# A hybrid attention and recurrence block: tables spread beside the recurrence, heads' weights split beside its last chunk, weights laid out by group

## The chip, the cores and the metric

The kernel runs on one core of a Trainium2 chip. The metric is the device time of one execution, in microseconds (us). TensorE (PE) does the matrix products, VectorE (DVE), ScalarE (ACT) and GpSimd (POOL) the elementwise work, and SyncE (SP) issues every DMA transfer of this kernel, on one queue. Each engine works through its own instructions in order; semaphores tie the engines together.

## What is computed

One block of a network acts on 2048 latent tokens (32 rows by 64 columns of a grid) and 256 context tokens, all of width 1024, in float32. Cut to its core:

```python
shift, scale, gate = split(silu(c) @ w_mod + b_mod, 3)      # same for the context, from c_ctx
h  = rms_norm(x, norm_g) * (1 + scale) + shift              # hc likewise
q, k, v, z_a, u, z_l = split(h @ w_in, ...)                 # w_in: 1024 x 3072, six groups of 512 columns
# group A: 8 heads of 64, neighbourhood attention (8 rows x 16 columns) plus all context keys
s_loc = where(col_mask, rope(norm(q)) @ rope(norm(k)) / 8 + rpb[head, dr, dc], -1e30)
attn  = softmax(concat[s_loc, norm(q) @ norm(k_ctx) / 8]) @ concat[v_band, v_ctx]
# group B: 8 blocks of 64, a convolution and a recurrence in both directions
uc = depthwise_conv(u) + conv_b
r, i = sigmoid(uc @ w_a + b_a), sigmoid(uc @ w_x + b_x)     # block-diagonal weights, per direction
a = exp(-8 * r * softplus(-lam)); b = sqrt(1 - a * a) * i * uc
y = scan(a, b, forward) + scan(a, b, backward)              # h_t = a_t * h_(t-1) + b_t
out = x + gate * (concat[attn * silu(z_a), y * silu(z_l)] @ w_out)
```

## The kernel before

Products that need float32 accuracy are made of float16 pairs: an operand is split into a high part (`hh`, `wh`) and a low part (`hl`, `wl`), and three products are added, high by high, low by high and high by low (L345 to L347 for channels by tokens, L604 to L606 for tokens by channels).

A weight group goes through two steps. `wload` brings 128 or 192 columns of `w_in` into a float32 tile `wraw` (L312, one DMA for each piece of columns, so three for a head's q, k and v). `wsplit` then finds its largest magnitude (a reduction on VectorE, L320, a transpose and a spread of it over the partitions by two small operations of TensorE, L112 and L115, with VectorE's L114 and L117 between), makes a power of two of it, and writes `wh` on ScalarE (L325) and `wl` on VectorE (L326).

The program runs in stages:

- The modulation vectors come from `w_mod`; then the context's 256 tokens and four blocks of 512 latent tokens are normalised, transposed on TensorE (L283), scaled on ScalarE into `h` (L286) and split into `hh` and `hl` (L288, L290).
- `tables` builds the attention's bias tables: the relative position bias `rp`, scaled, goes to DRAM (`d_r`, then `d_f`, which is first filled with the masking value NEG from the tile `ng`), comes back as `tu` and `tw`, is rearranged by ScalarE into `te` (L665 to L668) and written to DRAM as four tables `d_t`. From there 24 DMAs from DRAM to DRAM spread them into the three tables `d_e` that the heads read (L675), parts of which two DMAs fill with NEG (L677).
- `u_proj` makes the recurrence's input for a chunk of 128 channels, with the convolution (into `uc`).
- `lru` runs the recurrence for chunks 0 to 3. It loads the gates' weights into `gw` (L421, L424), splits them into `gh` and `gl` (L427, L428), and for each direction computes two gates for five stretches of tokens (three products each, L448 to L450, tanh at L452), the coefficients (L453 to L460) and the scans (L462, L469). `gw` takes one of two buffers of the tag "z", which the tiles `sz` of the next item use too.
- Beside each direction of a chunk, two of the four blocks of a z group are projected (`z_units`; tanh L480, `sz` L481, stored at L566 and L567) and, after the first direction, the next z group's weights are loaded and split. `gate` sums the output's gate vector from eight loads `wg` of `w_mod` (L584, L587, L589).
- After the last chunk the weights of heads 0 and 1 are loaded and split, head 0 is projected, and then the eight heads' attention runs, with the next head's projection beside it. The output projection ends the program.

The order of instructions on each engine isn't the order of the code: a scheduler places all instructions by a model of their times, by their dependences, and by priorities from the order in which the code issues them (`issue_after` makes what follows wait in that order for a given instruction). A DMA is placed on SP's queue in the same way. A transfer's semaphore is one of eight that are used in turn, so no more than eight transfers are outstanding.

Of the kernel before, what the change touches and what calls it, by code (L numbers as in the profile page):

```python
# [7 lines left out]
F32 = mybir.dt.float32  # L8
# [9 lines left out]
D = 1024  # L18
S = 2048
CTX = 256  # L20
NH = 8
HD = 64
AW = 512
LW = 512
KC = 8
# [3 lines left out]

NV = 5  # L30

CQ, CK, CV, CZA, CU, CZL = 0, 512, 1024, 1536, 2048, 2560

R_BM, R_G, R_C, R_CC, R_CW, R_CB, R_BA, R_BX, R_LAM, R_N = 0, 24, 32, 40, 48, 64, 68, 76, 84, 92
ROWS = ("b_mod", "norm_g", "c", "c_ctx", "conv_w", "conv_b", "lru_ba", "lru_bx", "lru_lam")
# [24 lines left out]
class K:  # L60
# [237 lines left out]
            return [self.wp["l"].tile([128, KC, 128], F16, tag=x, name=x, bufs=1) for x in ("wh", "wl")]  # L298
        return [self.wp["h"].tile([128, KC, 192], F16, tag=x, name=x, bufs=2)[:, :, 0:n] for x in ("wh", "wl")]

    def wload(self, parts, tag):

        n = sum(w for _, w in parts)
        wp = self.wp["z" if tag == "z" else "h"]
        if tag == "z":
            raw = (self.p0 or wp).tile([128, KC, n], F32, tag="raw", name="wraw", bufs=2 if self.p0 else 1)
        else:
            raw = wp.tile([128, KC, 192], F32, tag="raw", name="wraw", bufs=1)[:, :, 0:n]
        wv = self.a["w_in"].rearrange("(k p) n -> p k n", p=128)
        o = 0  # L310
        for c, w in parts:
            self.nc.sync.dma_start(raw[:, :, o:o + w], wv[:, :, c:c + w])  # L312
            o += w
        return raw, n, tag

    def wsplit(self, raw, n, tag, early=False):
# [13 lines left out]
        nc.vector.tensor_tensor(osc, inv, self.ial, ALU.mult)  # L330
        return wh, wl, osc

    def wgroup(self, parts, tag, slow=False, early=False):
        raw = self.wload(parts, tag)
        with ExitStack() as st:
            if slow:
                st.enter_context(self.tc.issue_after(self.hh_op.ins))
                st.enter_context(self.tc.issue_after(self.hl_op.ins))
            return self.wsplit(*raw, early)
# [72 lines left out]
    def lru(self, c, uc, p, fill):  # L412


        nc, a = self.nc, self.a
        N = CTX + S
        t = lambda x: p.tile([128, N], F32, tag=x, name=x, bufs=2)
        A, X = t("A"), t("X")
        gl = p.tile([128, 4, 128], F32R, tag="gl", name="gl", bufs=1)
        gw = self.zp.tile([128, 512], F32, tag="z", name="gw", bufs=2).rearrange("p (g c) -> p g c", g=4)  # L420
        nc.gpsimd.memset(gw, 0.0)  # L421
        for g, nm in enumerate(("lru_wa", "lru_wx")):
            for f in range(2):
                nc.sync.dma_start(gw[64 * f:64 * f + 64, 2 * g:2 * g + 2, 64 * f:64 * f + 64],  # L424
                                  a[nm][:, 2 * c + f].rearrange("d i j -> i d j"))
        gh = p.tile([128, 4, 128], F32R, tag="gh", name="gh", bufs=1)
        nc.vector.tensor_copy(gh, gw)  # L427
        nc.vector.tensor_tensor(gl, gw, gh.bitcast(F32), ALU.subtract)  # L428

        I = t("I")  # L430
        uh = p.tile([128, N], F32R, tag="uh", name="uh", bufs=1)
        ul = p.tile([128, N], F32R, tag="ul", name="ul", bufs=1)
        done = []
        for d in range(2):
            if d:
                A, X, I = t("A"), t("X"), t("I")
            kc = slice(4 * d + c, 4 * d + c + 1)
            for b in (0, CTX, CTX + 512, CTX + 1024, CTX + 1536):
                m = 512 if b else CTX
                s = slice(b, b + m)  # L440
                u = uc[:, s]
                if d == 0:
                    nc.scalar.copy(uh[:, s], u)  # L443
                    nc.gpsimd.tensor_tensor(ul[:, s], u, uh[:, s].bitcast(F32), ALU.subtract)  # L444
                for g, dst in enumerate((X, I)):
                    w = 2 * g + d
                    q = self.any_bank()[:, :m]
                    nc.tensor.matmul(q, gh[:, w, :], uh[:, s], start=True, stop=False)  # L448
                    nc.tensor.matmul(q, gh[:, w, :], ul[:, s], start=False, stop=False)
                    nc.tensor.matmul(q, gl[:, w, :], uh[:, s], start=False, stop=True)  # L450
                    k = 8 * g + 4 * d + c
                    nc.scalar.activation(dst[:, s], q, AF.Tanh, bias=self.hb[:, k:k + 1], scale=0.5)  # L452
                nc.vector.scalar_tensor_tensor(I[:, s], I[:, s], 1.0, u, ALU.add, ALU.mult)  # L453
            for h in range(2):
                s = slice(N // 2 * h, N // 2 * (h + 1))
                nc.scalar.activation(A[:, s], X[:, s], AF.Exp, bias=self.nk4[:, kc], scale=self.nk4[:, kc])
                nc.vector.scalar_tensor_tensor(I[:, s], A[:, s], 1.0, I[:, s], ALU.add, ALU.mult)
                nc.scalar.activation(X[:, s], X[:, s], AF.Tanh, bias=self.k2[:, kc], scale=self.k2[:, kc])
            nc.scalar.activation(X, X, AF.Sqrt, scale=0.25)
            nc.vector.tensor_tensor(X, X, I, ALU.mult)  # L460
            if d == 0:
                nc.vector.tensor_tensor_scan(A, A, X, 0.0, ALU.mult, ALU.add)  # L462
            done.append(A)
            fill(d)
        F, A = done
        init = 0.0
        for o, m in ((0, CTX), (CTX + S // 2, S // 2), (CTX, S // 2)):
            r = lambda x: x[:, o:o + m][:, ::-1]
            nc.vector.tensor_tensor_scan(r(A), r(A), r(X), init, ALU.mult, ALU.add)  # L469
            init = A[:, o:o + 1]  # L470
            if o:
                nc.gpsimd.tensor_tensor(F[:, o:o + m], A[:, o:o + m], F[:, o:o + m], ALU.add)
                nc.sync.dma_start(self.d_y[128 * c:128 * c + 128, o - CTX:o - CTX + m], F[:, o:o + m])
# [10 lines left out]
    def phase1(self, left, right):  # L484
        nc, a = self.nc, self.a
# [13 lines left out]
        with ExitStack() as s1:  # L499
# [2 lines left out]
            ug = {}  # L502

            def u_group(c, g=None):
                wh, wl, osc = g or self.wgroup([(CU + 128 * c, 128)], "z", slow=c > 1)
                if g:
                    osc = self.small(1, F32, "wo")
                    nc.vector.tensor_tensor(osc, g[2], self.ial, ALU.mult)
                cw = self.small(4, F32, f"cw{c % 2}")
                nc.vector.tensor_scalar(cw, self.vec[:, R_CW + c:R_CW + 16:4], osc, None, ALU.mult)  # L510
                return wh, wl, cw
# [10 lines left out]
            with ExitStack() as s0:  # L522
# [1 line left out]
                mods = self.mods(p0)  # L524
                next(mods)
                with self.tc.issue_after(self.last.ins):
                    g0 = self.wgroup([(CU, 128)], "z", early=True)
                xs = next(mods)
                with self.tc.issue_after(self.last.ins):
                    self.prep(p0, 2, 1, hhc, hlc, xs, True)  # L530
# [4 lines left out]
                    for tb in range(4):  # L535
# [1 line left out]
                        if tb < 3:  # L537
                            nxt = self.prep_in(p0, a["x"], 4, tb + 1)
                        self.prep(p0, 4, 0, self.hh[tb], self.hl[tb], xs)
                    with ExitStack() as s3:  # L540
                        self.tables(self.pool(s3, "tab", side="right"))
                    self.softplus(p0)
                    ucs = [u_proj(0), u_proj(1)]
# [3 lines left out]

            def z_group():
                c = len(za)
                g = self.wgroup([(CZA + 128 * c, 128)], "z", slow=c > 0)  # L550
                nc.vector.tensor_scalar(self.zs[:, c:c + 1], g[2], 0.5, None, ALU.mult)
                za.append(g)
            self.wp["h"] = self.pool(self.wright, "w2", bufs=2, side="right")
            with ExitStack() as s2:
# [4 lines left out]
                def z_units(c, d):  # L559
# [9 lines left out]
                    if d == 0 and c < 3:  # L569
                        z_group()  # L570

                for c in range(4):
                    self.lru(c, ucs[c], p, lambda d, c=c: z_units(c, d))
                    if c < 2:
                        ucs.append(u_proj(c + 2))

# [32 lines left out]
    def tables(self, q):  # L609
# [26 lines left out]
        nc.sync.dma_start(d_r, rp)  # L636
        d_f = self.drm.tile([16, 2, NH, 15, 32], F32, name="d_f")
        ng = q.tile([128, 864], F32, name="ng")
        nc.gpsimd.memset(ng, NEG)
        ff = d_f.rearrange("q t h k c -> (q t h k c)").rearrange("(p n) -> p n", p=128)  # L640
        for i in range(2):
            nc.sync.dma_start(ff[:, 480 * i:480 * i + 480], ng[:, 0:480])
# [7 lines left out]
        for t in range(3):  # L650
# [8 lines left out]
            for r in range(4):  # L659
                e = q.tile([128, 1024], F32, tag="te", name="te", bufs=2)  # L660
                for tab, o, g in ((u, 0, 5), (w, 640, 3)):
# [5 lines left out]
                    else:  # L667
                        nc.scalar.copy(eo, ti)  # L668
                nc.sync.dma_start(d_t[r][t], e)

        self.d_e = [self.drm.tile([2, NH, 64, 3, w], F32, name=f"d_e{i}") for i, w in enumerate(BW)]

        def spread(rt, f, r, o, src, n):
# [1 line left out]
            nc.sync.dma_start(e, d_t[r][:, :, src:src + n].rearrange("t p w -> p t w"))  # L675
        for f, o in ((0, 256), (1, 0)):
            nc.sync.dma_start(self.d_e[2 * f][f].rearrange("h (c r) t w -> (h c) (r t) w", r=4)[:, :, o:o + 128],  # L677
                              ng[:, 0:128].unsqueeze(1).broadcast_to([128, 12, 128]))
        for r in range(4):
            for f in range(2):  # L680
                spread(1, f, r, 0, 128 * (1 - f), 512)
# [1 line left out]
            spread(0, 0, r, 0, 768, 256)  # L683
            spread(2, 0, r, 0, 128, 384)
            spread(2, 1, r, 128, 640, 256)

    def bias_load(self, p, h, rt):

# [41 lines left out]
        self.nc.gpsimd.memset(v[:, :, 1, 64:66], 0.0)  # L730

    def head_w(self, n):
        return self.wload([(CQ + HD * n, HD), (CK + HD * n, HD), (CV + HD * n, HD)], "h")

    def head_bank(self, n):

# [185 lines left out]
    def phase2(self, left, right):  # L922
# [5 lines left out]
        with ExitStack() as sg:  # L928
# [13 lines left out]
                nc.gpsimd.memset(x[:, :, 64:128], 0.0)  # L942
            self.zero = self.const.tile([128, 1], F32, name="zero")
            nc.gpsimd.memset(self.zero, 0.0)
            self.hw, self.bias, self.o = {}, [], {}
            with self.tc.issue_after(self.last.ins):
                for i in range(2):
                    self.hw[i] = self.wsplit(*self.head_w(i))
                for H in self.head_proj(0, p, q):
                    pass  # L950
            lz = self.lru_gate()
# [23 lines left out]
    def lru_gate(self):  # L975

        nc = self.nc
        for c in range(4):
            hsc = self.zs[:, 4 + c:5 + c]

            raw = self.wload([(CZL + 128 * c, 128)], "h" if c == 3 else "l")
            yield
            wh, wl, osc = self.wsplit(*raw)
            nc.vector.tensor_scalar(hsc, osc, 0.5, None, ALU.mult)
# [158 lines left out]
```

## Time and profile before

| | us |
|---|---|
| median of 3 runs | 1267.96 (1267.69 to 1269.3) |
| the profiled execution | 1268.18 |
| its span | 1266.4 |
| TensorE busy | 1116.4 (88%) |
| VectorE busy | 926.4 (73%) |
| ScalarE busy | 618.0 (49%) |
| GpSimd busy | 472.2 (37%) |

The profile is of one execution. Its span runs from the first instruction to the last; 1.8 us of the measured time lie outside of it. A share of busy time is a mean over all stages, so a stage is read by its own stretch: normalising x from about 59 to 121 us, the first two `u_proj` to 150, the recurrence from 168 to about 420, head 0's projection to 460, attention and output to the end. `PEclk` is the granted clock of TensorE as a share of full speed.

### The profile page before, as it was taken

What the parts mean: (1) busy time and instruction counts of PE and PEld (TensorE: products, weight loads), DVE (VectorE), ACT (ScalarE), POOL (GpSimd) and SP (SyncE); (2) the same over time, 40 slices, a digit from 0 to 9 for tenths busy, and PEclk for the clock granted to TensorE, in tenths of its full rate; (3) what the DMA queues carried; (4) which work ended last, traced back from release to release, by engine and by line L of the source; (5) the groups of instructions that cost most, each with busy time, mean ns of one, the idle gap of its engine ahead of it and who ended that gap; (6) DMA issues with size and microseconds to landing.
All of it is one profiled execution on the core that took longest, in us unless ns stands there. A gap on an engine that the chain in (4) does not pass through costs nothing. (4 is left out here: it accounts for less than half of the span.)

```text
span 1266.4 us, 26204 instructions
## 1 busy us (share of the span) xinstructions
PE 1116.4 (88%) x9964; PEld 854.8 (67%) x9964; DVE 926.4 (73%) x2548; ACT 618.0 (49%) x1189; POOL 472.2 (37%) x861
## 2 busy tenths in 40 slices
PE   7767658996985959999999999999998997999997
PEld 1434324453543857899878988789887876888786
DVE  7898556869688667888978988788888874554432
ACT  1697118283588125655646555555555644231200
POOL 0245100403030377566564655646556462000000
PEclk9798869998998888999989999999999998999999
DMA  9746962111112623344533445335353537436352
GB/s 352 270 165 243 310 193 51 59 46 56 24 30 59 152 35 82 70 104 107 110 83 64 109 92 126 83 66 108 89 122 81 136 93 193 142 101 187 109 153 67
DMA packets 196014, 149.50 MB, mean 118 GB/s; under 512 B 129453, under 2 KB 168109, under 8 KB 195887
## 3 DMA queue, kind: packets, MB, share of 16 engines
q1 hardware_dynamic: 195887, 147.82, 43.6%
q8 instruction: 78, 1.28, 0.4%
q14 instruction: 49, 0.40, 0.1%
HBM read 96.42 MB, written 47.94 MB: 114 GB/s over the span
## 5 line engine op out<-in xcount | busy, mean ns | idle before, releaser
L604 PE MATMUL mm<-wh,hh 128*128 128x192 f16 x960 | 237.0, 247 | 1.7 <-DVE V L762 1.6
L605 PE MATMUL mm<-wl,hh 128*128 128x192 f16 x960 | 236.9, 247 | 0.0
L606 PE MATMUL mm<-wh,hl 128*128 128x192 f16 x960 | 236.9, 247 | 0.0
L895 DVE TENSOR_TENSOR Pl<-pt,Ph 128x384 f16<-128x384 f32 (+1 forms) x256 | 127.9, 517 | 57.2 <-ACT Ph L894 56.4
L345 PE MATMUL mm<-hh,wh 128*128 128x512 f16 x384 | 150.8, 393 | 17.9 <-DVE sz L481 12.0
L346 PE MATMUL mm<-hl,wh 128*128 128x512 f16 x384 | 150.0, 391 | 7.8 <-POOL hl L290 6.9
L887 ACT ACTIVATE SP<-SP,nb 128x640 f32<-128x640 f32 (+1 forms) x128 | 110.4, 880 | 94.2 <-DVE nb L885 89.8
L347 PE MATMUL mm<-hh,wl 128*128 128x512 f16 x384 | 148.7, 388 | 0.7 <-DVE wl L326 0.7
L894 ACT CAST Ph<-pt 128x384 f16<-128x384 f32 (+1 forms) x256 | 107.1, 452 | 79.2 <-PE pt L893 75.3
L893 PE MATMUL pt<-id,SP 128*128 128x128 f32 x704 | 116.9, 283 | 2.4 <-ACT SP L887 1.7
L604 PEld LDWEIGHTS <-hh 128*128 128x128 f16 x1024 | 100.6, 98 | 8.9 <-issue 5.2
L605 PEld LDWEIGHTS <-hh 128*128 128x128 f16 x1024 | 100.6, 98 | 2.8 <-issue 1.6
L606 PEld LDWEIGHTS <-hl 128*128 128x128 f16 x1024 | 100.5, 98 | 0.8
L882 DVE CUSTOM_DVE_ANT_0 SP<-sl,b,m 128x384 f32<-128x384 f32 (+1 forms) x128 | 93.4, 736 | 6.9 <-PE sl L830 6.2
L830 PE MATMUL sl<-qk,qt 128*128 128x128 f16 (+2 forms) x800 | 79.4, 232 | 17.9 <-DMA qk<-ST 8.2
L444 POOL TENSOR_TENSOR ul<-uc,uh 128x512 fp32r<-128x512 f32 (+1 forms) x20 | 30.5, 1553 | 151.0 <-ACT uh L443 150.9
L900 PEld LDWEIGHTS <-Ph 128*128 128x128 f16 x1408 | 79.5, 97 | 9.0 <-ACT Ph L894 2.9
L893 PEld LDWEIGHTS pt<-id,SP 128*128 128x128 f32 x704 | 79.4, 144 | 6.9 <-ACT SP L887 2.8
L346 PEld LDWEIGHTS <-wh 128*128 128x128 f16 x416 | 42.1, 101 | 59.2 <-issue 23.6
L347 PEld LDWEIGHTS <-wl 128*128 128x128 f16 x416 | 41.8, 101 | 56.9 <-issue 17.2
L719 POOL TENSOR_TENSOR ST<-P,ST 128x256 f16<-128x256 f32 x64 | 43.5, 680 | 93.7 <-ACT ST L718 93.4
L900 PEld LDWEIGHTS <-Pl 128*128 128x128 f16 x704 | 66.0, 99 | 17.1 <-DVE Pl L895 11.1
(303 smaller groups left out, 3049.5 us busy)
## 6 DMA issues: line engine op xcount, KB each, us to landing
b<-d_e SPq DMA_DIRECT2D x32, 288.0 KB
wm<-w_mod SPq DMA_DIRECT2D x16, 512.0 KB
x<-x SPq DMA_DIRECT2D x16, 512.0 KB
wraw<-w_in SPq DMA_DIRECT2D x12, 512.0 KB
d_t<-te SPq DMA_DIRECT2D x12, 512.0 KB
d_e<-d_t SPq DMA_DIRECT2D x8, 768.0 KB
wraw<-w_in SPq DMA_DIRECT2D x24, 256.0 KB
b<-d_e SPq DMA_DIRECT2D x16, 384.0 KB
```

What stands on the lines that cost most here:

```text
L345: nc.tensor.matmul(out, wh[:, k, :], hh[:, k, :n], start=(k == 0), stop=False)
L346: nc.tensor.matmul(out, wh[:, k, :], hl[:, k, :n], start=False, stop=False)
L347: nc.tensor.matmul(out, wl[:, k, :], hh[:, k, :n], start=False, stop=(k == KC - 1))
L604: nc.tensor.matmul(out, hh[:, k, t0:t0 + 128], wh[:, k, :], start=(k == 0), stop=False)
L605: nc.tensor.matmul(out, hh[:, k, t0:t0 + 128], wl[:, k, :], start=False, stop=False)
L606: nc.tensor.matmul(out, hl[:, k, t0:t0 + 128], wh[:, k, :], start=False, stop=(k == KC - 1))
L882: nc.vector.tensor_tensor_reduce(SP[:, 0:W], sl[:, 0:W], bt[:, CT[j], 0:W], self.qs, m1, ALU.add, ALU.max, accum_out=m2)
L887: nc.scalar.activation(SP[:, :N], SP[:, :N], AF.Exp, bias=nb)
L893: nc.tensor.transpose(pt[:, i - c0, :], SP[:, 128 * i:128 * i + 128], self.id32)
L894: nc.scalar.copy(Ph[:, c0:c1], pt)
L895: nc.vector.tensor_tensor(Pl[:, c0:c1], pt, Ph[:, c0:c1], ALU.subtract)
L900: nc.tensor.matmul(pv[:, jj], P[:, i, :], v[:, w:w + 66], start=(i == j0 == 0), stop=(i == nch - 1 and j0 == 2))
```

## The change

Four things change.

- `w_in` is handed over in two other layouts, `w_qkv` (a head's q, k and v columns together) and `w_gr` (the other groups of 128 columns), so that each load of a weight group is one DMA with one contiguous run for each partition.
- `tables` is issued behind x's last load. The masking value goes to a small DRAM tile `d_n`, from which the two NEG fills of `d_e` now read.
- The 24 spreads of `d_e` move out of `tables` into a generator of four parts of six, whose parts are issued beside the recurrence, at chunk 0's second direction, both of chunk 1 and the first of chunk 2 (the NEG fills stand at the first part). `gw` gets a buffer of its own.
- The weights of heads 0 and 1 are loaded and split beside chunk 3's two directions, no longer after the recurrence.

```diff
-    def wload(self, parts, tag):
+    def wload(self, src, tag):
...
-        wv = self.a["w_in"].rearrange("(k p) n -> p k n", p=128)
-        o = 0
-        for c, w in parts:
-            self.nc.sync.dma_start(raw[:, :, o:o + w], wv[:, :, c:c + w])
-            o += w
+        self.nc.sync.dma_start(raw, src)
...
-        gw = self.zp.tile([128, 512], F32, tag="z", name="gw", bufs=2).rearrange("p (g c) -> p g c", g=4)
+        gw = p.tile([128, 4, 128], F32, tag="gw", name="gw", bufs=1)
...
-                    with ExitStack() as s3:
+                    with ExitStack() as s3, self.tc.issue_after(self.xld.ins):
                         self.tables(self.pool(s3, "tab", side="right"))
...
+                self.hw = {}
+
+                spread = self.table_spread()
+
+                def fill(c, d):
+                    z_units(c, d)
+                    if (c, d) in ((0, 1), (1, 0), (1, 1), (2, 0)):
+                        next(spread)
+                    if c == 3:
+                        self.hw[d] = self.wsplit(*self.head_w(d))
+
                 for c in range(4):
-                    self.lru(c, ucs[c], p, lambda d, c=c: z_units(c, d))
+                    self.lru(c, ucs[c], p, lambda d, c=c: fill(c, d))
...
+        bneg = self.drm.tile([128, 128], F32, name="d_n")
         nc.gpsimd.memset(ng, NEG)
+        nc.sync.dma_start(bneg, ng[:, 0:128])
...
+    def table_spread(self):
+
+        nc, d_t = self.nc, self.d_t
         self.d_e = [self.drm.tile([2, NH, 64, 3, w], F32, name=f"d_e{i}") for i, w in enumerate(BW)]
...
-                              ng[:, 0:128].unsqueeze(1).broadcast_to([128, 12, 128]))
+                              self.bneg.unsqueeze(1).broadcast_to([128, 12, 128]))
         for r in range(4):
...
             spread(2, 1, r, 128, 640, 256)
+            yield
...
     def head_w(self, n):
-        return self.wload([(CQ + HD * n, HD), (CK + HD * n, HD), (CV + HD * n, HD)], "h")
+        return self.wload(self.a["w_qkv"][n], "h")
...
             with self.tc.issue_after(self.last.ins):
-                for i in range(2):
-                    self.hw[i] = self.wsplit(*self.head_w(i))
                 for H in self.head_proj(0, p, q):
```

The order of the instructions changes with it. First SP's queue, before the change, from the end of the spreads on (`d_e` is a spread, `wg` a load for the gate vector, `gw` the gates' weights, `wraw` a z group's weights):


```order
L675 DMA d_e_1027<-d_t_958 128x3x256
L584 DMA wg<-w_mod 128x1024 x2
L593 DMA grow<-b_mod 1x1024
L424 DMA gw<-lru_wa 64x2x64 x2
L424 DMA gw<-lru_wx 64x2x64 x2
L312 DMA wraw<-w_in 128x8x128
L584 DMA wg<-w_mod 128x1024 x6
L312 DMA wraw<-w_in 128x8x128
```

Here the gates' weights of chunk 0 and then z group 0's and 1's weights stand behind all 24 spreads. With the change SP's queue reads like this where the spreads begin,


```order
L678 DMA d_t_958<-te 128x1024
L688 DMA d_e_1810<-d_t_957 128x3x512
L420 DMA gw<-lru_wa 64x2x64 x2
L678 DMA d_t_959<-te 128x1024
L420 DMA gw<-lru_wx 64x2x64 x2
L678 DMA d_t_960<-te 128x1024
L688 DMA d_e_1810<-d_t_957 128x3x512
L688 DMA d_e_1809<-d_t_957 128x3x384
```

so that chunk 0's `gw` has one spread ahead of it, and like this where they end, with z group 1's weights in the last row:


```order
L688 DMA d_e_1810<-d_t_960 128x3x512
L591 DMA wg<-w_mod 128x1024
L688 DMA d_e_1809<-d_t_960 128x3x384
L688 DMA d_e_1809<-d_t_960 128x3x256
L688 DMA d_e_1811<-d_t_960 128x3x384
L688 DMA d_e_1811<-d_t_960 128x3x256
L309 DMA wraw<-w_gr 128x1024
```

All 24 spreads still stand ahead of z group 1's weights and of the first store of `sz`; z group 0's weights have moved up among them.

Next VectorE where the first z groups are done, before the change (`I` belongs to the recurrence, `sz` to z group 0, the reduction of `wraw` at L320 to z group 1):


```order
L589 SCALAR_TENSOR_TENSOR gacc<-wg,silu,gacc 128x1024
L551 TENSOR_SCALAR zs<-wo 128x1
L589 SCALAR_TENSOR_TENSOR gacc<-wg,silu,gacc 128x1024
L320 TENSOR_REDUCE wm<-wraw 128x1
L481 SCALAR_TENSOR_TENSOR sz<-sz,mm 128x512
L597 TENSOR_TENSOR grow<-grow,pt 1x512
L597 TENSOR_TENSOR grow<-grow,sc 1x512
L453 SCALAR_TENSOR_TENSOR I<-I,uc 128x256
L453 SCALAR_TENSOR_TENSOR I<-I,uc 128x512 x2
L114 TENSOR_REDUCE av<-po 1x1
L481 SCALAR_TENSOR_TENSOR sz<-sz,mm 128x512
L453 SCALAR_TENSOR_TENSOR I<-I,uc 128x512
```

And with the change, where the same steps have the lines L449, L477 and L316:


```order
L477 SCALAR_TENSOR_TENSOR sz<-sz,mm 128x512
L596 SCALAR_TENSOR_TENSOR gacc<-wg,silu,gacc 128x1024
L477 SCALAR_TENSOR_TENSOR sz<-sz,mm 128x512
L596 SCALAR_TENSOR_TENSOR gacc<-wg,silu,gacc 128x1024
L316 TENSOR_REDUCE wm<-wraw 128x1
L114 TENSOR_REDUCE av<-po 1x1
L477 SCALAR_TENSOR_TENSOR sz<-sz,mm 128x512
```

The steps of chunk 0's recurrence that stood between the `sz` are no longer there, and additions to `gacc` stand there instead; z group 1's reduction is still ahead of later `sz`, as it was.

Last TensorE at the end of the recurrence, before the change (L345 to L347 are the last z block, L112 and L115 belong to a head's split, L448 to L450 to the last gate, L604 on to head 0):


```order
L347 MATMUL mm<-hh_108,wl 128x512
L112 MATMUL mm<-id_63,wm 1x128
L448 MATMUL sc<-uh,gh 128x512
L449 MATMUL sc<-ul,gh 128x512
L450 MATMUL sc<-uh,gl 128x512
L115 MATMUL mm<-av,id_63 128x1
L604 LDWEIGHTS hhc
L604 MATMUL sl<-wh,hhc 128x128
L604 LDWEIGHTS hh_104
L604 MATMUL sl<-wh,hh_104 128x192
L605 LDWEIGHTS hhc
```

And with the change, where L343 is the end of the last z block and L611 to L613 are head 0:


```order
L343 LDWEIGHTS wl
L343 MATMUL mm<-hh_108,wl 128x512
L611 LDWEIGHTS hhc
L611 MATMUL sl<-wh,hhc 128x128
L612 LDWEIGHTS hhc
L612 MATMUL sl<-wl,hhc 128x128
L613 LDWEIGHTS hlc
L613 MATMUL sl<-wh,hlc 128x128
```

The split's two steps and the last gate's products are gone from between the last z block and head 0's projection; they stand further up.

## Rows read from the trace of the kernel before

**Rows 1.** Busy time (and count) of each engine in stretches of the span.

```profile
core 0: us, PE busy (x) PEld busy (x) DVE busy (x) ACT busy (x) POOL busy (x), PEclk, DMA share, GB/s
...
59.00:121.00 62.00, 44.05 (x224) 25.66 (x223) 53.88 (x96) 57.28 (x89) 29.95 (x24) 0.91 0.50 173
...
150.00:170.00 20.00, 1.36 (x4) 1.26 (x5) 7.06 (x11) 0.85 (x1) 0.00 (x0) 0.55 0.91 290
170.00:400.00 230.00, 199.42 (x887) 105.03 (x885) 173.79 (x206) 141.65 (x180) 43.74 (x24) 0.93 0.21 57
400.00:414.40 14.40, 1.00 (x4) 0.81 (x5) 13.93 (x18) 11.42 (x11) 0.00 (x0) 0.53 0.09 18
...
460.00:480.00 20.00, 8.05 (x58) 5.86 (x56) 9.99 (x44) 7.28 (x16) 15.97 (x36) 0.66 0.23 46
```

**Rows 2.** TensorE's waits, 140 to 420: who is waited for, us, times, longest.

```profile
PE sl L448 <- DVE gh L427: 22.0, 2, 20.1
PE mm L345 <- DVE sz L481: 12.0, 3, 5.8
PE po L115 <- DVE av L114: 7.5, 1, 7.5
PE mm L115 <- DVE av L114: 7.3, 1, 7.3
PE sl L604 <- ACT wh L325: 4.5, 1, 4.5
...
PE sl L605 <- DVE wl L326: 2.6, 1, 2.6
```

**Rows 3.** TensorE's times: start, us, instruction, idle before it and its releaser.

```profile
148.15 0.38 PE L115 MATMUL po<-av,id 1*128 1x1 f32 x2
168.64 0.58 PE L448 MATMUL sl<-uh,gh 128*128 128x256 f32 x1 [20.12 <-DVE gh L427]
...
178.58 0.39 PE L345 MATMUL mm<-hh,wh 128*128 128x512 f16 x1 [1.67 <-ACT wh L325]
...
398.77 0.40 PE L450 MATMUL sc<-uh,gl 128*128 128x512 f32 x1
...
414.49 0.26 PE L605 MATMUL sl<-wl,hhc 128*128 128x128 f16 x1 [2.56 <-DVE wl L326]
```

**Rows 4.** VectorE's times, at four places.

```profile
168.16 0.42 DVE L427 CAST gh<-gw 128x512 fp32r<-128x512 f32 x1
...
169.23 1.21 DVE L320 TENSOR_REDUCE wm<-wraw 128x1 f32<-128x1024 f32 x1
...
207.34 0.68 DVE L481 SCALAR_TENSOR_TENSOR sz<-sz,mm 128x512 f32<-128x512 f32 x1
...
423.38 0.27 DVE L771 TENSOR_TENSOR rgc<-sl,gs 128x128 f32<-128x128 f32 x1
```

**Rows 5.** SP's times of issue, 0 to 480; the last column is the count.

```profile
49.56 0.35 SPq L636 DMA_DIRECT2D d_r<-rp  x1
...
117.96 36.56 SPq L675 DMA_DIRECT2D d_e<-d_t  x19
...
160.51 3.06 SPq L424 DMA_DIRECT2D gw<-lru_wx  x2
...
180.66 0.38 SPq L312 DMA_DIRECT2D wraw<-w_in  x1
```

**Rows 6.** The spreads, from the view of tile d_e: ns, least, median, most.

```profile
L675 SPq DMA_DIRECT2D d_e<-d_t x24: 618/1690/4050, 111.0 to 152.7; - x24
```

**Rows 7.** ScalarE's times, first h of x and first copy into te.

```profile
58.94 0.78 ACT L286 ACTIVATE h<-pt,sha,Ga 128x512 f32<-128x512 f32 x1 [1.66 <-PE pt L283]
...
73.00 2.57 ACT L668 COPY te<-tu 128x640 f32<-128x640 f32 x2
```

**Rows 8.** VectorE's wl of a head, 400 to 480, groups by form: busy us, mean ns.

```profile
L326 DVE SCALAR_TENSOR_TENSOR wl<-wraw,ws,wh 128x1536 f16<-128x1536 f32 x2 | 3.6, 1817 | 0.3 <-ACT wh L325 0.3
```

More of the change, by code (lines that the diff above doesn't have):

```diff
@@ L30 @@
 NV = 5
-CQ, CK, CV, CZA, CU, CZL = 0, 512, 1024, 1536, 2048, 2560
+GZA, GU, GZL = 0, 4, 8
 R_BM, R_G, R_C, R_CC, R_CW, R_CB, R_BA, R_BX, R_LAM, R_N = 0, 24, 32, 40, 48, 64, 68, 76, 84, 92
@@ L299, in w_tiles @@
         return [self.wp["h"].tile([128, KC, 192], F16, tag=x, name=x, bufs=2)[:, :, 0:n] for x in ("wh", "wl")]
-    def wload(self, parts, tag):
-        n = sum(w for _, w in parts)
+    def wload(self, src, tag):
+        n = src.shape[2]
         wp = self.wp["z" if tag == "z" else "h"]
@@ L331, in wsplit, with wgroup @@
         return wh, wl, osc
-    def wgroup(self, parts, tag, slow=False, early=False):
-        raw = self.wload(parts, tag)
+    def wgroup(self, g, tag, slow=False, early=False):
+        raw = self.wload(self.a["w_gr"][g], tag)
         with ExitStack() as st:
@@ L504, in u_group @@
             def u_group(c, g=None):
-                wh, wl, osc = g or self.wgroup([(CU + 128 * c, 128)], "z", slow=c > 1)
+                wh, wl, osc = g or self.wgroup(GU + c, "z", slow=c > 1)
                 if g:
@@ L526, in phase1 @@
                 with self.tc.issue_after(self.last.ins):
-                    g0 = self.wgroup([(CU, 128)], "z", early=True)
+                    g0 = self.wgroup(GU, "z", early=True)
                 xs = next(mods)
@@ L549, in z_group @@
                 c = len(za)
-                g = self.wgroup([(CZA + 128 * c, 128)], "z", slow=c > 0)
+                g = self.wgroup(GZA + c, "z", slow=c > 0)
                 nc.vector.tensor_scalar(self.zs[:, c:c + 1], g[2], 0.5, None, ALU.mult)
@@ L669, in tables @@
                 nc.sync.dma_start(d_t[r][t], e)
+        self.d_t, self.bneg = d_t, bneg
+    def table_spread(self):
+        nc, d_t = self.nc, self.d_t
         self.d_e = [self.drm.tile([2, NH, 64, 3, w], F32, name=f"d_e{i}") for i, w in enumerate(BW)]
@@ L979, in lru_gate @@
             hsc = self.zs[:, 4 + c:5 + c]
-            raw = self.wload([(CZL + 128 * c, 128)], "h" if c == 3 else "l")
+            raw = self.wload(self.a["w_gr"][GZL + c], "h" if c == 3 else "l")
             yield
@@ L1117 @@
         "x": (S, D), "ctx": (CTX, D),
-        "w_mod": (D, 3 * D), "b_mod": (24, 128), "w_in": (D, 3 * D), "w_out": (D, D),
+        "w_mod": (D, 3 * D), "b_mod": (24, 128), "w_out": (D, D),
         "q_norm_g": (1, HD), "k_norm_g": (1, HD), "rpb": (NH * 15, 31),
@@ L1123 @@
     arrays["vec"] = np.ascontiguousarray(np.concatenate([np.asarray(inputs[n]).reshape(-1, 128) for n in ROWS]).T)
+    w = np.asarray(inputs["w_in"]).reshape(KC, 128, 3 * D).transpose(1, 0, 2)
+    arrays["w_qkv"] = np.ascontiguousarray(w[:, :, :3 * AW].reshape(128, KC, 3, NH, HD).transpose(3, 0, 1, 2, 4).reshape(NH, 128, KC, 3 * HD))
+    arrays["w_gr"] = np.ascontiguousarray(w[:, :, 3 * AW:].reshape(128, KC, 12, 128).transpose(2, 0, 1, 3))
     half = HD // 4
```

2 lines of the change are left out of this document (1 added, 1 removed).

## The prediction, made before the changed kernel had run

> **What bounds the kernel now.** I read the stretch table first, to see which engine is idle where the change works [rows 1]. From 59 to 121 us, where x is normalised, ScalarE is busy 57.28 of 62.00 us: that stretch is ScalarE's. From 150 to 170 TensorE works 1.36 us of 20.00 while the DMA engines are 0.91 busy: a wait on transfers. From 170 to 400 TensorE is busy 199.42 of 230.00, VectorE 173.79, ScalarE 141.65: mostly TensorE's, with 30.6 us of holes. From 400 to 414.4 TensorE does 1.00 us and VectorE 13.93 of 14.40.
>
> The list of TensorE's waits names these holes [rows 2]: 22.0 us for the gates' weights gh (one wait of 20.1), 12.0 for the z blocks' sz, 7.5 and 7.3 at the two ends of the weights' maximum (L115), 4.5 and 2.6 for head 0's wh and wl. TensorE's own times [rows 3] place them: nothing between L115 at 148.15 and the first gate at 168.64; nothing of size between the last gate at 398.77 and head 0's stream at 414.49. SP's times give the reason for the first [rows 5]: 19 spreads are issued from 117.96 on over 36.56 us, and gw's second pair goes out only behind them, at 160.51. VectorE casts it at 168.16 [rows 4]. From 460 to 480 TensorE is again idle 12 us.
>
> **Terms, part by part.**
>
> *Tables behind x's loads.* Two moves oppose each other. x is no longer behind the tables' transfers, so the ScalarE-bound stretch, whose first h is now at 58.94 [rows 7], can begin about 7 us earlier: the four NEG fills that were issued ahead of most of x carry 2.06 MB, 7 us at 290 GB/s [rows 1]. But the table chain starts later. Its first link, d_r, was issued at 49.56, and the first copy into te came at 73.00, 23.4 us behind [rows 5, 7]; now that copy stands in ScalarE's order after block 1's h, and the chain's links come behind all of x. The copies are the same, so ScalarE's sum does not change; what it gains by starting it loses by waiting at the first te. I take 0, between −7 (no wait) and +14 (a wait of 21 us, nearly the chain's whole length, less the 7). The transfer that now carries NEG through DRAM is one of 64 KB on a queue that is not waited for: 0.
>
> *gw in a buffer of its own, its load ahead of the spreads.* The wait of 20.1 goes [rows 2, 3]: −20.1. uc and uh of the context block are ready before, since TensorE's queue named gh alone. gh waited twice, 22.0 in all; the second, 1.9, is of the same kind: −1.9. Together −22.0, and at the least −12 if the next operand is 10 us late.
>
> *What is late next.* The gates now stand together on TensorE and z block 0 behind them. Its weights' split (maximum, L112, L115, wh, wl) had gates around it before: its reduction started at 169.23 [rows 4] and z's first matmul at 178.58 [rows 3], 9.35 us with 24 gates in between. Now those gates are finished when the split runs, in a queue that is served in order. Between 0 (the split overlaps the gates as before) and +9.4 (all bare), I take the middle, +5.
>
> *Spreads beside the recurrence.* The 24 spreads stay on the one SP queue and now stand among gw, wg and the z weights. At 36.56/19 = 1.92 us each [rows 5] they take 46 us; with six 512 KB loads between them, at 290 GB/s [rows 1] about 1.8 us each, 57 us. From about 120 (when the last d_t is written) z block 1's weights land near 177 to 183, where they were issued at 180.66 before [rows 5]. VectorE has z 1's reduction ahead of z 0's third sz. By the terms above VectorE is there near 174 (gates from 148.5, 8 us; split 5; two blocks of 24 matmuls and their sz, 12). It then waits 3 to 9 us, and TensorE, which has one free bank, a part of that. I take +3, between 0 and +9.
>
> *Middle of the recurrence.* No operation is added; 30.6 us of TensorE's holes bound a gain [rows 1], and the order is another. I take 0, between −15 (half the holes) and +15 (as much new).
>
> *Heads' split beside chunk 3.* TensorE's waits of 7.3, 4.5 and 2.6 [rows 2] go, as head 0's weights are ready: from the last gate's start, 398.77, plus 0.4, to 414.49 are 15.3 us [rows 3], −15.3. VectorE could hold that back: it is nearly full there, and reads the first head's sums only at 423.38 [rows 4], behind the scans. What it sheds for certain are the two wl, 3.6 us [rows 8]; that is the least, −4. The most is the 15.3 and the 12 idle us of 460 to 480: −27. The nearest rows are TensorE's own, so −15.3. The moved split's cover is VectorE's 56 idle us of 170 to 400; were there none, it would cost its own 3.6 and the two reductions' about as much.
>
> *Weights by group.* 15 fewer DMAs and longer runs. Of TensorE's waits none names a weight load [rows 2]: 0, at best −2.
>
> Sum: 0 − 22.0 + 5 + 3 + 0 − 15.3 = −29.3. The profiled execution took 1268.18 us, 1.8 of it outside the span; the median of the runs is 1267.96, so 0.2 less changes nothing. Forecast **1239**.
>
> A rule weighed: the clock. In 150 to 170 and 400 to 414.4 the granted clock was 0.55 and 0.53 [rows 1], near the lower level (1.2 of 2.4 GHz), after TensorE had stood still; the first gate, of 256 columns, took 0.58 us where a late one, of 512, took 0.40 [rows 3]. The Trainium skill, "TensorE: Matmul & The Clock Gate", Part 1, says that the gate falls to half rate when the array idles and that work opens it again. By it the gates and head 0's first stream, no longer behind a hole, would run at the full rate: the 24 gates some 3 us sooner, and the sum would be 1236. I leave it out, as the split's bare wait makes a hole of its own.
>
> **Rivals.**
>
> *B, the start is given back: 1253.* If the recurrence is paced by VectorE and ScalarE with their waits, starting it 20 us sooner only lets it wait for z 1's and gacc's loads behind the spreads. Only the tail's 15.3 is left: 1268.2 − 15.3. For it: 12.0 us of waits for sz, VectorE's 174 of 230. Against it: TensorE waited for gh with nothing else to do, and all later work stands behind.
>
> *C, the holes close too: 1216 to 1224.* gw out of sz's buffers leaves sz two of its own, and the waits of 12.0 and 7.5 go with the first: half of 30.6, −15, gives 1224; the clock of 460 to 480 8 more, 1216. Against it: sz's waits may come from VectorE's order.
>
> *D, slower: 1273.* z 1's weights starve behind the spreads. One spread took up to 4.05 us, the median 1.69 [rows 6]. At 4.05 for all, 24 take 97 us, with the loads 107, so z 1's weights land at 227; VectorE, with z 0's third sz behind that wait, was there at 207.34 before [rows 4]. That is 20 late, less the tail's 15.3, or +5. It decides from a mean of 3.8 us (120 + 11 + 24 × 3.8 = 222, where the loss equals the tail). Against it: they average 1.92 on a queue already full. The Trainium skill, "DMA: Bandwidth & Descriptors", Queues, rings and completion order, says that each engine takes descriptors in the ring's order; what is issued behind the spreads is then served behind them, and the trace agrees as far as gw goes, cast at 168.16 after an issue at 160.51.
>
> *E, nothing: 1267.* Half of the table chain's wait stands bare in ScalarE's stretch (+7), z 0 and z 1 take their full prices (+9 each), the tail gives only VectorE's 4 and the gates 22: −1. In this case the loads change places, and what they were moved for does not come. For it: ScalarE has no idle time there to hide a wait in, and VectorE none at the tail. Against it: all of these bounds would have to hold at once.
>
> **Chances.** Forecast 50% (own range 1228 to 1250), B 20%, C 18%, D 6%, E 6%. A measurement tells 0.2%, 2.5 us, from no change. Faster: A, B, C and a part of E, 0.90; same 0.04; slower, D, 0.06. The range 1212 to 1260 leaves out D, E and the far ends.
>
> **What would show it.** The list of TensorE's waits without gh's 20.1 and the granted clock of the following 20 us higher; first gate near 148 (front term: earlier or later); z 0's matmuls about 5 us behind the last gate; VectorE waiting for wraw ahead of z 0's third sz by under 9 us; head 0's stream within 1 us of the last z matmul. Wrong: a ScalarE wait at te of over 10 us, or spreads with a mean above 3 us, or a recurrence of more than 245 us from first gate to last.

## The result, and the profile after

The changed kernel takes 1254.04 us (median of 4, 1251.45 to 1256.14); the kernel before, run again beside it, 1267.83 (1266.71 to 1269.3). The ratio is 0.9885, with a 95% interval of 0.9858 to 0.9913: 14 us faster. The profiled execution took 1252.79 us with a span of 1251.0, 15.4 us shorter than before. The forecast was 1239. The sign held, and the time lies inside the wide range of 1212 to 1260, but 4 us outside the forecast's own range of 1228 to 1250: the gain was half of what was forecast.

The stretches of [rows 1], in the kernel after:

```profile
59.00:121.00 62.00, 42.60 (x195) 23.48 (x195) 53.32 (x117) 45.23 (x72) 25.28 (x22) 0.78 0.45 149
150.00:170.00 20.00, 12.73 (x46) 6.21 (x47) 9.81 (x20) 4.28 (x6) 0.00 (x0) 0.83 0.97 319
170.00:400.00 230.00, 193.32 (x874) 106.07 (x872) 178.67 (x213) 148.44 (x184) 46.45 (x23) 0.92 0.26 80
400.00:414.40 14.40, 14.40 (x167) 14.09 (x164) 14.06 (x21) 2.31 (x5) 8.04 (x29) 0.93 0.27 92
460.00:480.00 20.00, 17.70 (x203) 14.94 (x202) 14.48 (x58) 11.99 (x29) 16.60 (x34) 0.91 0.40 100
```

From 150 to 170 TensorE works 12.73 us, not 1.36, and from 400 to 414.4 all the time: the second hole is filled, and most of the first. But in between it is busy 193.32 of 230, less than the 199.42 before.

TensorE's longest waits, as in [rows 2]:

```profile
PE po L112 <- DVE wm L316: 12.2, 4, 4.6
PE sl L444 <- ACT uh L439: 11.8, 2, 7.0
PE sl L445 <- POOL ul L440: 5.7, 2, 4.0
PE mm L341 <- DVE sz L477: 3.6, 4, 2.2
PE sl L444 <- ACT X L448: 2.7, 1, 2.7
```

The wait for gh is gone, and of the two of over 7 us for L115 0.7 us is left. In their place are waits for a weight's maximum (L316), for chunk inputs (uh, ul) and for a tanh. Those named are 36 us together.

TensorE's times at the places of [rows 3], and more:

```profile
148.46 0.47 PE L444 MATMUL sl<-uh,gh 128*128 128x256 f32 x1
...
159.74 0.58 PE L112 MATMUL po<-id,wm 128*1 128x128 f32 x2 [4.64 <-DVE wm L316]
...
163.28 0.61 PE L341 MATMUL mm<-hh,wh 128*128 128x512 f16 x1 [2.00 <-ACT wh L321]
...
168.59 0.38 PE L341 MATMUL mm<-hh,wh 128*128 128x512 f16 x1
...
205.39 1.02 PE L603 MATMUL pt<-gacc,gone 128*1 128x512 f32 x2
...
207.20 0.39 PE L444 MATMUL pt<-uh,gh 128*128 128x256 f32 x1
...
393.97 0.22 PE L611 MATMUL sl<-wh,hhc 128*128 128x128 f16 x1
```

The first gate is at 148.46, 20.2 us earlier than in [rows 3]. z group 0 starts at 163.28, 15.3 earlier. The next place was not in the rows before the prediction: the gate vector's two products (L603, which sum `gacc` over the partitions) take the banks pt and sc at 205.39, and the first gate on pt stands right behind, at 207.20. The same pair in the kernel before:

```profile
190.06 1.02 PE L596 MATMUL pt<-gacc,gone 128*1 128x512 f32 x2
...
191.87 0.38 PE L448 MATMUL pt<-uh,gh 128*128 128x256 f32 x1
```

VectorE's times in the kernel after, the places that answer to [rows 4] among them:

```profile
176.96 1.28 DVE L596 SCALAR_TENSOR_TENSOR gacc<-wg,silu,gacc 128x1024 f32<-128x1024 f32 x1 [4.77 <-DMA wg<-w_mod]
...
187.55 1.22 DVE L316 TENSOR_REDUCE wm<-wraw 128x1 f32<-128x1024 f32 x1 [5.97 <-DMA wraw<-w_gr]
...
199.68 1.28 DVE L596 SCALAR_TENSOR_TENSOR gacc<-wg,silu,gacc 128x1024 f32<-128x1024 f32 x1 [2.71 <-DMA wg<-w_mod]
...
230.08 5.49 DVE L458 TENSOR_TENSOR_SCAN A<-A,X 128x2304 f32<-128x2304 f32 x1
...
413.71 0.28 DVE L785 TENSOR_TENSOR rgc<-sl,gs 128x128 f32<-128x128 f32 x1
```

It waits 4.77 us for the third slice of `wg`, 5.97 for z group 1's weights, and makes the last sum of `gacc` at 199.68. Chunk 0's first scan comes at 230.08; before, it came at 213.82:

```profile
213.82 4.95 DVE L462 TENSOR_TENSOR_SCAN A<-A,X 128x2304 f32<-128x2304 f32 x1
```

So a recurrence whose first gate is 20 us earlier starts its first chunk's forward scan 16 us later. SP's times give the loads' places:

```profile
164.87 1.94 SPq L591 DMA_DIRECT2D wg<-w_mod  x1
...
177.69 1.13 SPq L309 DMA_DIRECT2D wraw<-w_gr  x1
...
194.64 0.43 SPq L591 DMA_DIRECT2D wg<-w_mod  x1
```

The third `wg` is issued at 164.87 among the spreads, z group 1's weights at 177.69, the last `wg` at 194.64, behind stores of `sz`. Before, the last six `wg` were issued between 166.18 and 179.7, in one row of SP's:

```profile
166.18 13.55 SPq L584 DMA_DIRECT2D wg<-w_mod  x6
```

The spine of the program, in us from the span's start (each the start of an instruction in that kernel's trace; the kernels below the second are the experiments):

| | first gate | gate vector's products | first scan | fourth scan | head 0's first product | first score | span |
|---|---|---|---|---|---|---|---|
| before | 168.6 | 190.1 | 213.8 | 399.4 | 411.5 | 466.3 | 1266.4 |
| the change | 148.5 | 205.4 | 230.1 | 383.4 | 394.0 | 448.3 | 1251.0 |
| spreads behind wg | 142.6 | 160.5 | 186.2 | 362.0 | 377.1 | 422.6 | 1225.9 |
| products from two slices | 146.0 | 152.4 | 187.5 | 358.8 | 373.9 | 419.6 | 1227.9 |
| split back, in the change | 147.2 | 203.8 | 228.5 | 382.0 | 404.9 | 455.3 | 1246.0 |
| split alone, in before | 169.1 | 189.0 | 212.8 | 399.3 | 395.9 | 455.7 | 1254.0 |
| split back, spreads behind wg | 140.8 | 158.8 | 184.3 | 362.1 | 387.2 | 439.6 | 1238.6 |
| gw shared | 187.1 | 201.3 | 225.5 | 413.2 | 409.1 | 469.1 | 1264.9 |

### The profile page after: what moved, and what is told of

It reads as the page before. It is cut to its first block, busy times and chain, and to the rows that moved or that the text cites. A ratio compares the mean times of both kernels' runs of the same rounds, so it can differ in the third digit from the quotient of the medians.

```text
span 1251.0 us, 26168 instructions
## 1 busy us (share of the span) xinstructions
PE 1120.3 (90%) x9964; PEld 856.5 (68%) x9964; DVE 922.3 (74%) x2548; ACT 616.5 (49%) x1189; POOL 475.2 (38%) x861
## 5 line engine op out<-in xcount | busy, mean ns | idle before, releaser
L611 PE MATMUL mm<-wh,hh 128*128 128x192 f16 x960 | 238.2, 248 | 0.9 <-DVE V L776 0.8
L613 PE MATMUL mm<-wh,hl 128*128 128x192 f16 x960 | 237.9, 248 | 0.0
L342 PE MATMUL mm<-hl,wh 128*128 128x512 f16 x384 | 149.3, 389 | 10.6 <-POOL hl L290 7.4
L343 PE MATMUL mm<-hh,wl 128*128 128x512 f16 x384 | 148.5, 387 | 0.0
L611 PEld LDWEIGHTS <-hh 128*128 128x128 f16 x1024 | 100.9, 99 | 3.1 <-DVE V L776 1.0
L613 PEld LDWEIGHTS <-hl 128*128 128x128 f16 x1024 | 100.8, 98 | 0.8
L343 PEld LDWEIGHTS <-wl 128*128 128x128 f16 x416 | 41.5, 100 | 59.0 <-issue 18.2
L342 PEld LDWEIGHTS <-wh 128*128 128x128 f16 x416 | 41.7, 100 | 53.5 <-issue 15.9
L844 PEld LDWEIGHTS <-qt 128*128 128x128 f16 x800 | 59.0, 100 | 27.9 <-issue 18.3
L914 PEld LDWEIGHTS <-Pl 128*128 128x128 f16 x704 | 66.0, 99 | 17.6 <-DVE Pl L909 12.3
```

What stands on the lines that cost most here:

```text
L342: nc.tensor.matmul(out, wh[:, k, :], hl[:, k, :n], start=False, stop=False)
L343: nc.tensor.matmul(out, wl[:, k, :], hh[:, k, :n], start=False, stop=(k == KC - 1))
L611: nc.tensor.matmul(out, hh[:, k, t0:t0 + 128], wh[:, k, :], start=(k == 0), stop=False)
L613: nc.tensor.matmul(out, hl[:, k, t0:t0 + 128], wh[:, k, :], start=False, stop=(k == KC - 1))
L844: self.nc.tensor.matmul(out, lq, k(x[:, i]), start=(i == 2), stop=(i == 3))
L914: nc.tensor.matmul(pv[:, jj], P[:, i, :], v[:, w:w + 66], start=(i == j0 == 0), stop=(i == nch - 1 and j0 == 2))
```

## The experiments

**Why the first scan is late.** The first two put the spreads behind other loads, so that these land early. Spreads behind the gate vector's last load:

```diff
-            nc.sync.dma_start(w, wm[k, :, 2 * D:])
+            self.wgd = nc.sync.dma_start(w, wm[k, :, 2 * D:])
...
-                        next(spread)
+                        with self.tc.issue_after(self.wgd.ins):
+                            next(spread)
```

Expected: 

> The changed kernel with one order added: the spreads are issued behind the last of the gate vector's eight loads (wg). Theory 1, the gate vector stands in the recurrence's way: in the changed kernel its loads land behind the spreads, its last sum is at 199.7 us, its two products take the banks pt and sc that the ninth gate needs, and chunk 0's first scan comes at 230.1 where it was at 213.8 before. Then the first scan comes before 210, and the kernel takes 1240 us (1234 to 1246). Theory 2, the recurrence is paced by the sum of its work (from the first gate to head 0's first product are 243 us before and 246 after, whatever stands in between): 1254 us, within 3.

Measured: 1227.9 us, ratio to before 0.9686 (0.965 to 0.9722), some 26 us below the changed kernel and below all that theory 1 expected. SP's queue shows the loads ahead of the spreads, and TensorE the two products, 45 us earlier:

```profile
145.70 9.45 SPq L592 DMA_DIRECT2D wg<-w_mod  x4
...
157.67 22.54 SPq L689 DMA_DIRECT2D d_e<-d_t  x13
```

```profile
160.54 1.86 PE L604 MATMUL pt<-gacc,gone 128*1 128x512 f32 x2 [3.71 <-DVE gacc L597]
...
164.04 0.58 PE L444 MATMUL pt<-uh,gh 128*128 128x256 f32 x1
```

The first scan is at 186.2. From the first gate to head 0's first product are 234.4 us; they were 242.9 before and 245.5 after the change. So it is not the sum of its work that sets the recurrence's length: theory 2 falls.

Spreads behind z group 1's load (`issue_after` on that load instead). Expected: 

> The changed kernel, with the spreads issued behind z group 1's weight load, so behind the gate vector's loads too. Theory 1: as with the spreads behind wg, and VectorE's wait of 5.97 us for z group 1's weights goes as well: 1237 us (1231 to 1243). Theory 2: 1254 us, within 3. A third, that the spreads' traffic must be paid wherever it stands (46 us of the queue, then beside chunk 0's stores and the next weights): 1250 to 1260, with waits for wraw or d_z of over 5 us later on.

Measured: 1233.05 us, 0.9715 (0.9686 to 0.9745). Theory 1's time, but not below the first experiment: the intervals overlap. The pair doesn't price the wait for z group 1's weights, as with the spreads behind wg VectorE waited only 0.19 us for them.

Both move transfers as well as the order on TensorE. The next one leaves SP's order as it was up to z group 1's weights (issued at 178.67, 177.69 in the changed kernel; behind them the order differs), and changes only what the two products wait for. It makes the two products right after the second slice (the lines for `one`, `row` and the products move there, unchanged); the other six slices are loaded and multiplied, but left out of the gate vector:

```diff
-            else:
-                nc.vector.scalar_tensor_tensor(acc, w, s, acc, ALU.mult, ALU.add)
+            elif k == 1:
+                nc.vector.scalar_tensor_tensor(acc, w, s, acc, ALU.mult, ALU.add)
...
+            else:
+                nc.vector.scalar_tensor_tensor(w, w, s, acc, ALU.mult, ALU.add)
```

Expected: 

> The changed kernel, its transfers and its spreads left where they are; only the gate vector's two products are made from the first two of the eight slices (all eight are still loaded and multiplied, the other six sums are left out of the result). So the banks pt and sc come free early, while the late landings behind the spreads stay. Theory 1a, the banks: chunk 0's first scan comes before 205 us (230.1 in the changed kernel) and the kernel takes 1236 us (1230 to 1244). Theory 1b, the late landings themselves (VectorE's waits of 4.8, 1.5 and 6.0 us for wg and wraw) hold the recurrence: 1250, within 4.

Measured: 1228.45 us, 0.9692 (0.9667 to 0.9716), as fast as with the spreads moved. The products and the first gate on pt:

```profile
152.45 1.86 PE L603 MATMUL pt<-gacc,gone 128*1 128x512 f32 x2 [5.09 <-DVE gacc L596]
...
155.95 0.58 PE L444 MATMUL pt<-uh,gh 128*128 128x256 f32 x1
```

With 1b it should have stayed near 1250. The slices land as late as before (the third is issued at 163.85, the last at 199.36), but nothing urgent waits for them: the scheduler puts the last six sums behind other work, and of VectorE's waits for `wg` and `wraw` between 150 and 235 us none is over 1.1 us. So it is what the products wait for: in the code they take two of the banks that the gates use, in the rotation (sl, pt, sl, pt, sc), ahead of the gates; `sc` has one buffer and `pt` two, and a buffer is free only when its last user has been read. In the changed kernel the eight gates on sl ran at once and all others stood behind the products, whose last slice of `wg` had come behind the spreads and stores and was summed at 199.68. Through the products the late landing costs 25.6 us (1254.04 − 1228.45).

The other traces bear this out. In all twelve the first gate on pt stands behind the two products. In eleven of them the first scan starts 23.8 to 25.8 us after the first product, wherever the first gate is (136.2 to 187.1); with the products from two slices it is 35.0. Two things stay open: why the first gate on pt does not take the second buffer of pt sooner, and what the kernel does with the products in banks of their own, which no run tried.

**What the heads' split is worth.** Put back behind the recurrence in the changed kernel, and moved alone in the kernel before:

```diff
-                    if c == 3:
-                        self.hw[d] = self.wsplit(*self.head_w(d))
...
             with self.tc.issue_after(self.last.ins):
+                for i in range(2):
+                    self.hw[i] = self.wsplit(*self.head_w(i))
```

Expected of the first: 

> The changed kernel with the heads' split put back behind the recurrence. By the prediction's term the move was worth 15.3 us: 1269 us. By the two traces, in which head 0's stream starts 20.5 us earlier but the last gate only 12.6, it is worth about 8: 1262 us. If VectorE bounds the tail, 4: 1258 us.

Measured: 1250.15 us, 0.9847 (0.982 to 0.9874): not slower than with the move. None of the three expected that. The table shows two parts: the first score comes 7.0 us later (455.3 for 448.3), but from there to the end are 790.7 us, where the changed kernel has 802.7 and the kernel before 800.1. The scheduler ordered the eight heads otherwise. Why that order is 12 us shorter was not settled. Over all twelve traces this stretch takes 790.7 to 808.3 us though of the edits only the weights' layout reaches into it, so a difference of a few us between two whole times says little on the part that was edited.

Expected of the second: 

> The kernel before, with only the heads' split moved beside chunk 3 (weights in the old layout, three loads to a head). By the prediction's term: 1252.5 us. By the two traces, 8 us: 1260. If VectorE bounds the tail, 4: 1264. Nothing, if the split's work on VectorE delays chunk 3 by as much as it saves: 1268.

Measured: 1254.44 us, 0.9876 (0.9845 to 0.9907), 13.4 us faster, near the prediction's term, and at the first score 10.6. A third run put the split back in the kernel with the spreads behind wg. Expected: 

> The kernel with the spreads behind the gate vector's loads, with the heads' split put back behind the recurrence. The split's move cost 4 us in the changed kernel (1254 with it, 1250 without) and gave 13 in the kernel before. If it is worth what it gave there: 1241 us. If the tail is VectorE's (4 to 5 us at the first score): 1233. If it is worth nothing or less, as in the changed kernel: 1224 to 1228.

Measured: 1240.24 us, 0.979 (0.9759 to 0.9822), so the move is worth 12.3 us there, and 17.0 at the first score. TensorE's waits in that kernel between 360 and 400:

```profile
PE sl L610 <- ACT wh L321: 7.4, 1, 7.4
PE sl L611 <- DVE wl L322: 4.2, 1, 4.2
PE mm L115 <- DVE av L114: 2.1, 1, 2.1
```

They sum to 13.7, and are of the kind that [rows 2] showed.

**The other parts.** `gw` back in the buffers that it shared with `sz`:

```diff
-        gw = p.tile([128, 4, 128], F32, tag="gw", name="gw", bufs=1)
+        gw = self.zp.tile([128, 512], F32, tag="z", name="gw", bufs=2).rearrange("p (g c) -> p g c", g=4)
```

Expected: 

> The changed kernel with gw back in the buffers that it shared with sz. Its loads then stand behind 20 of the 24 spreads in SP's order. If gw's place is what the change gained by (the prediction's 22 us): the first gate after 160 us and 1270 us or more. If the order around the gate vector decides (its products now stand ahead of most of z's): 1254, within 6.

Measured: 1267.89 us, 1.0003 (0.9984 to 1.0021): nothing is left of the whole change's gain, though it is not the 1270 or more of the first theory. `gw` is issued behind the spreads again,

```profile
131.19 24.89 SPq L688 DMA_DIRECT2D d_e<-d_t  x13
...
172.18 2.13 SPq L420 DMA_DIRECT2D gw<-lru_wa  x2
```

and TensorE stands at z group 0's split and starts the gates at 187, later than before:

```profile
172.56 0.58 PE L112 MATMUL po<-id,wm 128*1 128x128 f32 x2 [25.48 <-DVE wm L316]
...
187.05 0.47 PE L444 MATMUL sl<-uh,gh 128*128 128x256 f32 x1
```

But the late first gate is not where the time goes. The first gate is 38.6 us later than in the changed kernel, and the first scan 4.6 us earlier, as the products stand 4.1 us earlier. The loss comes behind it: the fourth scan is 29.8 us later. There chunk 1's gates' weights are cast long after the first scan, and in the changed kernel ahead of it. The first row is from the kernel with `gw` shared, the second from the changed one:

```profile
265.32 0.42 DVE L423 CAST gh<-gw 128x512 fp32r<-128x512 f32 x1
...
222.49 0.43 DVE L423 CAST gh<-gw 128x512 fp32r<-128x512 f32 x1 [0.86 <-PE sc L445]
```

Whether that cast is the cause was not tested.

The old weight layout (`wload` with pieces of `w_in`, as in the diff's removed lines), in the kernel with the spreads behind wg. Expected: 

> The kernel with the spreads behind the gate vector's loads, but with the weights in the old layout (12 loads of 512-byte runs, three loads to a head). The prediction put the layout at 0, at best 2 us: 1228 to 1230 us. If the short runs lengthen loads that the engines wait for: 1232 to 1238.

Measured: 1229.89 us, 0.9719 (0.9705 to 0.9734), against 1227.9, 0.9686 (0.965 to 0.9722). The medians differ by 2 us and the intervals overlap, so no effect is shown. In the profiled executions the first score comes at 428.8, 6.2 later than in the base, so one of some us isn't excluded.

The tables ahead of x again (`issue_after(self.xld.ins)` taken off), same base. Expected: 

> The kernel with the spreads behind the gate vector's loads, but the tables issued without regard to x's loads, as before. The prediction put that edit at 0, between -7 and +14 in time, so undoing it gives 1228 us, between 1214 and 1235; u_proj's end at 148 us in both traces speaks for 1228, within 4. If the tables' fills ahead of x delay its first blocks by 7 us: 1235.

Measured: 1224.73 us, 0.9678 (0.9664 to 0.9692): the lowest median of all kernels, 3 us below 1227.9 with overlapping intervals. Its first gate is at 136.2, its fourth scan at 353.5 and its first score at 422.9, where the base has 142.6, 362.0 and 422.6: what the front gains is lost ahead of the first score.

Last, the same with the spreads behind z group 1's load. Expected: 

> The kernel with the tables issued as before and the spreads behind z group 1's weight load. With the spreads behind the gate vector's loads alone VectorE still waits 6.4 us at once for a z group's weights, and 15.4 in all. If that wait is on the path: 1219 us. If the recurrence fills it with other work: 1225, within 2. If the spreads then meet the later stores and loads: 1228 to 1232, as the move behind z group 1's load cost 5 us with the tables behind x.

Measured: 1224.85 us, 0.9676 (0.9632 to 0.9719): no difference, though VectorE's waits for the loads of `w_gr` between 130 and 400 us fell from 15.4 to 5.0. First the run above, then this one:

```profile
DVE wm L316 <- DMA wraw<-w_gr: 15.4, 5, 6.4
...
DVE wm L316 <- DMA wraw<-w_gr: 5.0, 4, 2.8
```

So the wait of 6.4 us for a z group's weights is not on the path in these kernels.

## Why the prediction was half right

- *Tables behind x, 0.* Right in size. x's first h is 6.3 us earlier than in [rows 7], and ScalarE then waits at the first te; the copy is 15.9 us later:

```profile
52.63 0.78 ACT L286 ACTIVATE h<-pt,sha,Ga 128x512 f32<-128x512 f32 x1 [0.39 <-PE pt L283]
...
88.89 2.52 ACT L677 COPY te<-tu 128x640 f32<-128x640 f32 x2 [4.04 <-DMA tu<-d_f]
```

  The wait was 4.04 us, and u_proj ended at 148 us, as before. The run without the edit puts it at 3 us of loss or nothing.
- *gw, −22.0.* The wait went as forecast, and the first gate moved by 20.2 us, but that gain was not passed on: at the first scan the change is 16.3 us behind. Without the buffer the whole gain is gone, but by what the table shows it is lost behind the first scan, where the prediction's term is 0.
- *z group 0's split bare, +5.* Right: the 24 products of the eight gates on sl were done, and TensorE waited 4.64, 0.37 and 2.00 us for its maximum, its spread and wh, 7.0 in all.
- *Spreads, +3.* The mechanism was right, with VectorE waiting 5.97 us (3 to 9 forecast) and TensorE 3.0 at L112. But the term looked at the wrong load. z group 1's weights were late, and where the runs shortened such waits it gained nothing; the gate vector's slices, which the term counted only as traffic among the spreads, were late and cost 25.6.
- *Middle of the recurrence, 0.* This is the step whose mechanism failed. "No operation is added" was true, but the order on TensorE put all of z group 0 and most of a u projection ahead of the ninth gate, and the prediction took an order that it had read as neutral. Behind it is a chain over three engines: SP's queue, `wg`, `gacc` on VectorE, the two products, the banks pt and sc, the gates. The row at 190.06 in the trace of before showed its end, one row ahead of the gates on pt. That the sum still came out here is luck: from the first gate to the first scan the change loses 36.4 us (45.2 became 81.6), and from there to the fourth scan it regains 32.3 (185.6 became 153.3). So at the fourth scan it is 16.0 us ahead, where the terms up to there give 14.
- *Heads' split, −15.3.* Near, with 13.4 in the kernel before and 12.3 with the spreads behind wg. In the changed kernel itself the time shows none of it: without the move it is 3.9 us shorter, with intervals that overlap. From the fourth scan to the first score the change takes 64.9 us, before 66.9; undoing the move costs 7.0 at the first score, and the stretch behind it gives more than that back. So along the table this is the term that is missing in the time, and why is open. VectorE held part of it back, as the lower bound had it: head 0's products start 17.5 us earlier, but its first sums are read at 413.71, 9.7 earlier than in [rows 4].
- *Layout, 0 to −2.* Nothing speaks against it; the run does not settle it.
- *The clock.* With no hole ahead, the granted clock of 150 to 170 was 0.83 for 0.55, and the first gate took 0.47 us for 0.58. The Trainium skill, "TensorE: Matmul & The Clock Gate", Part 1, says that the gate is at half rate when the array has idled and that work opens it; the trace agrees. The 24 products of the first eight gates took 6.6 us for 8.3, in which two small operations of the split stood too. But behind the split's wait of 7.0 us z group 0's first products took 0.61 us for 0.38, so the prediction's reason for leaving the clock out held.

Rival B had the time, 1253, and named the gate vector's loads behind the spreads, but its parts were the other way round: it gave the start back and kept the tail, and along the table the change keeps 16.0 us at the fourth scan and gains nothing behind it. Nor is the work of VectorE and ScalarE what holds the recurrence: with the spreads behind wg the same work, from the first gate to head 0's first product, takes 11.1 us less. Of rival C, TensorE's waits for sz did fall, from 12.0 to 3.6 us, but others came in their place. D's point of decision, spreads of 3.8 us each, was not reached: their median was 0.75, the longest 2.79.

With the products early the change is worth 38 us (1228 against 1267), against the 29 of the forecast. The further 9 may come from the same chain, which stood in the kernel before too: there the products were at 190.06 and the first scan at 213.8, and with them at 152 to 161 it is at 184 to 188. No run took it out of the kernel before alone.

## What to carry to other kernels

When a change reorders DMA queues, follow each load that moved back to its last reader and then to what that reader holds: a buffer or PSUM bank whose turn comes ahead of the critical work makes an unimportant sum critical. The chain is found in the order by looking for the one stranger among the users of a rotating buffer. Load such work early, or give it a place behind (which no run here tried); here one line that set the queue's order was worth nearly twice the change itself. And follow the time along the stages, not only to the end: here an early first gate, a late first scan and a shorter stretch behind it added up to the forecast's sum at the fourth scan.

## Not expected

VectorE operations on 128x1 elements, which take 0.14 to 0.16 us, took 1.46 and 2.20 us beside two GpSimd additions of 128x1024 elements. VectorE's rows and then GpSimd's, in the kernel after:

```profile
407.67 0.14 DVE L106 TENSOR_SCALAR wi<-p 128x1 int32<-128x1 int32 x1
407.84 1.46 DVE L326 TENSOR_TENSOR wo<-wi,ial 128x1 f32<-128x1 f32 x1
409.34 0.16 DVE L760 RECIPROCAL ep<-wo 128x1 f32<-128x1 f32 x1
409.42 2.20 DVE L765 TENSOR_TENSOR vcf<-wo,zs 128x1 f32<-128x1 f32 x1
411.54 0.15 DVE L762 TENSOR_TENSOR ep<-ep 128x1 f32<-128x1 f32 x1
```

```profile
404.97 6.63 POOL L468 TENSOR_TENSOR A<-A 128x1024 f32<-128x1024 f32 x2 [36.94 <-issue]
```

Long and short ones alternate within the same 6.6 us. The two long ones are of the kind that reads two tiles (TENSOR_TENSOR), the short ones beside the additions read one; a TENSOR_TENSOR at 411.54, as the additions end, took 0.15 us. The two long ones add 3.4 us to VectorE's order ahead of head 0's first sums. No run was made on this.
